# Products on constants ahead of the first projections: five before the first transposes, twenty-four in place of fourteen, and seven more between the turns of the first tile

## The chip, the cores and the metric

The kernel runs on one core of one Trainium2 chip. The metric is the device time of one execution in microseconds (us). A core has five engines that run their own instruction queues: TensorE (PE, whose weight loads stand apart as PEld), VectorE (DVE), ScalarE (ACT), GpSimd (POOL) and SyncE (SP). SP here does nothing but issue loads and stores. Instructions of different engines wait for each other through semaphores.

## The reference

One layer of a decoder trunk, with 512 positions and 1024 channels, in fp32. Cut to what matters here:

```python
cs = jax.nn.silu(c)
mod = cs @ w_ada[l] + b_ada[l]
shift1, scale1, gate1, shift2, scale2, gate2 = ... jnp.split(mod, 6, axis=-1)

h = _rmsnorm(x, norm1_g[l]) * (1.0 + scale1) + shift1
proj = h @ w_in[l]
qa, ka, va, qd, kd, vd, ga, gd = jnp.split(proj, points, axis=-1)
out_a = _sliding_window_attention(qa, ka, va, swa_sinks[l], slopes_swa)
out_d = _diff_attention(qd, kd, vd, lam, lam_init, diff_subln_g[l], slopes_diff)
merged = sigmoid(ga) * (out_a @ w_branch_swa[l]) + sigmoid(gd) * (out_d @ w_branch_diff[l])
x = x + gate1 * (merged @ w_out[l])

h2 = _rmsnorm(x, norm2_g[l]) * (1.0 + scale2) + shift2
x = x + gate2 * _conv_ffn(h2, w_up[l], conv_w[l], conv_b[l], w_down[l])
return _rmsnorm(x, final_g)
```

`mod` is a product of one row with a 1024 x 6144 matrix. The change lies ahead of the first 768 columns of `h @ w_in`, which are `qa`, `ka` and `va`.

## The kernel before

**Products.** An fp32 operand is split in two parts, high and low, of the type fp32r; a product is made of three: high x high, low x high, high x low. ScalarE makes the high part by a copy, VectorE the low part by a subtraction. So each weight that is loaded costs one instruction on ScalarE and one on VectorE: `w0h` and `w0l` (L297 to L306) for the first projections, `w_h` and `w_l` (L115, L116) for those of the heads.

**PSUM** is given out from pools: two banks "f", three "s", two "t" and one "v". The six accumulators of the first projections, `acc6`, take two f, three s and the v. `acc6[5]` is the v.

**The start** (L230 to L415) stands under a manual schedule for VectorE, ScalarE and TensorE: their instructions keep the order in which they are written. SP's queue is ordered by the scheduler, by times that it plans. Step by step:

- `crow`, eight rows of `c`, is loaded and transposed on TensorE (L164); `cs = silu(c)` follows on ScalarE and VectorE (L232 to L235).
- `rows` (the bias of the modulation, the gains of the norms) comes through ScalarE's queue and is transposed on TensorE (L237).
- `keep_warm(WARM)` (L337 to L342): 14 products of `ident` and `ones` into `acc6[5]`, which the first real product overwrites. No one reads them.
- `ac_ops` (L246 to L258): VectorE sums the columns of `w_ada`, each of its eight row blocks times a column of `cs`, into two halves `ac`, and adds the two (L258). `reduce_mod` (L260 to L268) sums over the partitions on TensorE: `pa`, four matmul records. `finish_mod` (L270 to L278) makes the scale and shift `mod` of 128 channels from it (L274, L277).
- `stat`, `normalise`, `turn` for the four row tiles of x: sum of squares on ScalarE (L349), the reciprocal root on VectorE and GpSimd (L169 to L183), the scaling of the first 256 channels (L356), and the transposition of the first 128 channels on TensorE (L361). Behind the first three turns stands a `keep_warm(3)` each, behind the first one also `finish_mod(0, reduce_mod(0))`.
- `h_tile` (ScalarE, L318) applies `mod` to the transposed tile, `h_low` (VectorE, L322) makes its low part.
- The loop over eight groups of 128 channels of h: `mm_k` (L324 to L334) has three parts of six products. While group g is multiplied, VectorE and ScalarE prepare group g+1: its weights (`split_hi`, `split_lo`), its column sums and `mod`, its turn and tile of h. `pa` of the next group stands on TensorE ahead of the third part.

**Behind it** (`man.close()`, L416) TensorE alone keeps a written order. VectorE, ScalarE and SP are ordered by the scheduler, by the times that it plans and by priorities. What runs there first:

- the accumulators are taken out as `qa` (ScalarE L431, VectorE L432), `ka` (L428, L429) and `vaT`;
- `lp`, `ls`, `nlam` (L460 to L464) and `nsink` (L466), small ones on VectorE, from the loads `lamv` and `sink`; `cv` (L454) from the transposed `crow` of the convolution;
- `load_cols` (L469 to L472) loads the heads' weights `w` and splits them;
- `ada_rows` (L757 to L785) makes the other four rows of modulation: 32 loads `ra` of 512 KB through SP, two instructions `arow` on VectorE for each (L776 for the first of a row, else L778). The next load is asked for ahead of the sums over the last one, and the loads share four raw buffers with `w`. A row goes through TensorE and ScalarE (`row`, L794) and GpSimd's queue to memory;
- the sliding-window branch, by pairs of heads: scores on TensorE (`sw`), `st` with the maxima on VectorE (L561), `nm` (L572), exponentials on ScalarE (L573 to L577), `lsum` and the scaling of `st` on VectorE (L580 to L584), transposes `tp` (L595) and values `oa` on TensorE. Scores and softmax have a high priority; the sums `arow` have half of it from a certain step of the order on.

After that come the differential branch, the output projection, and the gated MLP, where TensorE works without long pauses up to the end.

Of the kernel before, what the change touches and what calls it, by code (L numbers as in the profile page):

```python
# [14 lines left out]
P = 128  # L15
# [20 lines left out]
NORM_LAG = 16  # L36
SWA_FILL = (2, 2, 5, 2, 2, 2, 2, 3)
DIFF_FILL = (3, 2, 4, 2)
WARM = 14
GROUPS = ((0,), (1,), (2,), (3,), (4,), (5,), (6,), (7,))  # L40
AC_CUT = 7
MOD_AT = 2
# [11 lines left out]
def kernel(  # L54
# [22 lines left out]
    nc = tc.nc  # L77
# [12 lines left out]
    def bank(tag, bufs, shape, name, dt=F32):  # L90
        return ps.tile(shape, dt, tag=tag, bufs=bufs, name=name)
# [7 lines left out]
    def tbank(name, shape=(P, S)):  # L99
        return bank("t", 2, list(shape), name)  # L100
# [28 lines left out]
    ident = cpool.tile([P, P], F32, name="ident")  # L129
    make_identity(nc, ident)  # L130
    ones = cpool.tile([P, P], F32, name="ones")
# [96 lines left out]
    acc6 = {i: (fbank, sbank, vbank)[(0, 0, 1, 2, 1, 1)[i]](f"a{i}") for i in DONE}  # L228
# [5 lines left out]
    nc.vector.reciprocal(cs, cs)  # L234
    nc.vector.tensor_mul(cs, cs, pc8)  # L235
    pc = tbank("pc", (P, NR))
    nc.tensor.transpose(pc, rows, ident[:NR, :NR])  # L237
    cols = cpool.tile([P, NR], F32, name="cols")
    nc.vector.tensor_copy(cols, pc)
# [6 lines left out]
    def ac_ops(gi, lo, hi):  # L246
        g = groups[gi]
        if lo == 0:
            ac[gi] = [pp.tile([P, 2, len(g) * P], F32, tag=f"ac{b}", bufs=2, name=f"ac{gi}_{b}") for b in range(2)]
        aw = adaw[g[0]]  # L250
        for kk in range(lo, hi):
            a = ac[gi][kk % 2]
            if kk < 2:
                nc.vector.tensor_scalar_mul(a, aw[:, :, kk], cs[:, kk : kk + 1])
            else:
                nc.vector.scalar_tensor_tensor(a, aw[:, :, kk], cs[:, kk : kk + 1], a, ALU.mult, ALU.add)
        if hi == KT:
            nc.vector.tensor_add(ac[gi][0], ac[gi][0], ac[gi][1])  # L258

    def reduce_mod(gi):  # L260
        pas = []
        for i, k in enumerate(groups[gi]):
            pa = tbank(f"pa{k}", (P, 2))
            for j in range(2):
                nc.tensor.matmul(
                    pa[:, j : j + 1], ac[gi][0][:, j, i * P : (i + 1) * P], ones[:, 0:1], start=True, stop=True
                )
            pas.append(pa)  # L268
        return pas

    def finish_mod(gi, pas):
        for k, pa in zip(groups[gi], pas):
            m = pp.tile([P, 16], F32, tag="mod", bufs=3, name=f"mod{k}")
            nc.vector.scalar_tensor_tensor(  # L274
                m[:, 0:1], pa[:, 0:1], bsc1[:, k : k + 1], n1g[:, k : k + 1], ALU.add, ALU.mult
            )
            nc.vector.tensor_add(m[:, 1:2], pa[:, 1:2], bsh[:, k : k + 1])  # L277
            mods[k] = m  # L278

    def w0_views(k):  # L280
        wh, wl = wts[k]
        return [
            a.rearrange(f, **n)
            for a, f, n in (
                (w0[k][:, 0:512], "p (a i d) -> p i a d", dict(a=2, i=4)),
                (wh[:, 0:512], "p (i a d) -> p i a d", dict(i=4, a=2)),
                (wl[:, 0:512], "p (i a d) -> p i a d", dict(i=4, a=2)),
            )
        ]

    def split_hi(k):
        pl, nb = (wp, WB) if k % 2 == 0 else (pp, 2)
        wh = pl.tile([P, 768], F32R, tag="whi", bufs=nb, name=f"w0h{k}")
        wl = pl.tile([P, 768], F32R, tag="wlo", bufs=nb, name=f"w0l{k}")
        wts[k] = (wh, wl)
        rq, wq, lq = w0_views(k)
        nc.scalar.copy(wq, rq)  # L297
        nc.scalar.copy(wh[:, 512:768], w0[k][:, 512:768])

    def split_lo(k, part):  # L300
        wh, wl = wts[k]
        if part == 0:
            rq, wq, lq = w0_views(k)
            nc.vector.tensor_tensor(lq, rq, wq.bitcast(F32), ALU.subtract)
        else:
            nc.vector.tensor_sub(wl[:, 512:768], w0[k][:, 512:768], wh[:, 512:768].bitcast(F32))  # L306
# [8 lines left out]
    def h_tile(k):  # L315
        hf = pp.tile([P, S], F32, tag="hf", bufs=2, name=f"hf{k}")
        for dst in (hTh[k], hf):
            nc.scalar.activation(dst, pts[k], AF.Identity, bias=mods[k][:, 1:2], scale=mods[k][:, 0:1])  # L318
        hfs[k] = hf
# [13 lines left out]
                    acc6[i], lhs[:, i * P : (i + 1) * P], rhs[k], start=k == 0 and p == 0, stop=last and p == 2  # L333
                )  # L334


    def keep_warm(n):  # L337
        for i in range(n):
            nc.tensor.matmul(acc6[5][:, :P], ident, ones, start=True, stop=True)

    keep_warm(WARM)
    ac_ops(0, 0, KT)  # L342
    rst = pp.tile([P, NT], F32, name="rst")
    half = [None] * NT

    def stat(t):
        sq = pp.tile([P, D], F32, tag="sq", bufs=1, name=f"sq{t}")
        ss = pp.tile([P, 1], F32, tag="ss", bufs=4, name=f"ss{t}")
        nc.scalar.activation(sq, xn[:, t], AF.Square, accum_out=ss)  # L349
        half[t] = rstd_start(ss, 1, D, pp)  # L350
# [3 lines left out]
    def normalise(t):  # L354
        rstd_end(rst[:, t : t + 1], *half[t], 1, pp)
        nc.vector.tensor_scalar_mul(xn[:, t, :HEAD], xn[:, t, :HEAD], rst[:, t : t + 1])  # L356
# [3 lines left out]
    def turn(t):  # L360
        nc.tensor.transpose(pts[0][:, t * P : (t + 1) * P], xn[:, t, 0:P], ident)  # L361

    for t in range(NT):
        stat(t)
        if t:
            normalise(t - 1)
            turn(t - 1)
            keep_warm(3)
        if t == 1:
            finish_mod(0, reduce_mod(0))  # L370
    split_hi(0)
    normalise(NT - 1)
    turn(NT - 1)
    h_tile(0)
    split_lo(0, 0)
    split_lo(0, 1)
# [491 lines left out]
    for s in range(4 * DIFF_HEADS):  # L868
        h, n = divmod(s, NT)
# [947 lines left out]
```

## Time and profile before

| what | value |
|---|---|
| median of 3 runs | 703.3 us (701.72 to 703.88) |
| the profiled execution's own time | 702.35 us |
| its span in the profile | 700.5 us |
| mean granted TensorE clock | 0.995 |
| loads `ra`, median from issue to landing | 3.9 us |

A line of the timeline gives the start, the duration, the engine, the line of the code, the operation, what it writes and reads, and in brackets the idle time ahead of it on its engine with what ended it. A line that stands for several instructions has their number at its end. Times begin with the span. A granted clock of 1.00 is the full clock of TensorE. An engine's idle time costs something only where the chain of waits that sets the end runs through it.

### The profile page before, as it was taken

The numbers are of one execution on the slowest core, as the hardware profiler recorded it, in microseconds if no ns is written. First come the engines' busy times: TensorE is split into PE (matmuls) and PEld (weight loads), VectorE is DVE, ScalarE is ACT, GpSimd is POOL, SyncE is SP. The second block draws the span as 40 slices with busy tenths as digits, with TensorE's granted clock in tenths as the row PEclk, the third lists the DMA queues.
The fourth block names the chain that finished last, engine by engine and source line by source line (L and its number), as shares of the span: only waits on it lengthen the run. The fifth ranks groups of instructions, "written<-read, shape, count | busy, mean of one in ns | idle before, by whom it ended". The sixth has DMA issues, their size and how long they took to land.

```text
span 700.5 us, 11253 instructions
## 1 busy us (share of the span) xinstructions
PE 682.6 (97%) x4203; PEld 595.0 (85%) x4203; DVE 573.1 (82%) x1100; ACT 375.1 (54%) x666; POOL 82.4 (12%) x100
## 2 busy tenths in 40 slices
PE   6999999999999999999999999999999999999995
PEld 5777777777788888888889999999999999888884
DVE  5999886887985656663589999888888999979996
ACT  4646666454552333332468656655555666656664
POOL 3000000000001000000030111112111102540300
PEclk9999999999999999999999999999999999999998
DMA  9995454354535676239717788786889738997903
GB/s 313 289 273 159 149 152 151 98 173 121 140 102 160 207 232 185 91 99 281 251 39 144 151 200 199 174 209 184 209 213 217 173 129 219 191 198 196 166 1 120
DMA packets 115862, 121.81 MB, mean 174 GB/s; under 512 B 4383, under 2 KB 93280, under 8 KB 115808
## 3 DMA queue, kind: packets, MB, share of 16 engines
q1 hardware_dynamic: 96894, 95.09, 43.4%
q0 software_dynamic: 18720, 25.73, 22.0%
q8 instruction: 33, 0.54, 0.3%
q10 hardware_dynamic: 194, 0.28, 0.1%
q14 instruction: 21, 0.17, 0.1%
HBM read 118.97 MB, written 2.11 MB: 173 GB/s over the span
## 4 chain that ended last, share of the span: by engine, by line
PE 75%; DVE 13%; DMA 4%; ACT 4%; issue 2%; SPq 0%; POOL 0%; POOLq 0%; ACTq 0%
PE up L1152 26%; PE dc L1761 13%; DMA ra<-in_w_ada_dram 4%; PE a L332 3%; PE pgd L119 2%; PE oc L1208 2%; PE oc L1212 2%; PE pgd L121 2%; PE oc L1209 2%; PE pgd L120 2%; PE pga L119 2%; PE pga L121 2%; PE pga L120 2%; DVE arow L778 1%; DVE m_wlo L1097 1%
## 5 line engine op out<-in xcount | busy, mean ns | idle before, releaser
L1152 PE MATMUL up<-t,m_whi 128*128 128x256 f32 x528 | 96.2, 283 | 0.0
L1152 PEld LDWEIGHTS up<-t,m_whi 128*128 128x128 f32 x528 | 82.3, 192 | 0.0
L1152 PE MATMUL up<-t,m_wlo 128*128 128x256 f32 x264 | 74.7, 284 | 0.5 <-DVE m_wlo L1097 0.5
L1152 PE MATMUL up<-bh,p_wlo 128*128 128x256 f32 x232 | 65.6, 283 | 0.1
L1152 PE MATMUL up<-bh,p_whi 128*128 128x256 f32 x232 | 65.6, 283 | 0.0
L1152 PE MATMUL up<-bl,p_whi 128*128 128x256 f32 x232 | 65.6, 283 | 0.0
L778 DVE SCALAR_TENSOR_TENSOR arow<-ra,cs,arow 128x512 f32<-128x512 f32 x56 | 41.9, 749 | 21.0 <-DMA ra<-in_w_ada_dram 20.5
L1152 PEld LDWEIGHTS up<-t,m_wlo 128*128 128x128 f32 x264 | 50.6, 192 | 0.9 <-DVE m_wlo L1097 0.9
L1152 PEld LDWEIGHTS up<-bh,p_wlo 128*128 128x128 f32 x232 | 44.5, 192 | 0.3 <-DVE p_wlo L1097 0.3
L1152 PEld LDWEIGHTS up<-bl,p_whi 128*128 128x128 f32 x232 | 44.5, 192 | 0.0
L1152 PEld LDWEIGHTS up<-bh,p_whi 128*128 128x128 f32 x232 | 44.5, 192 | 0.0
L1065 POOL DMA_DIRECT2D s<-in_w_up_dram x21 | 27.0, 1360 | 143.1 <-DMA s<-in_w_up_dram 54.2
L1097 DVE TENSOR_TENSOR m_wlo<-s,m_whi 128x1024 fp32r<-128x1024 f32 x31 | 37.7, 1217 | 0.9 <-ACT m_whi L1093 0.9
L1093 ACT CAST m_whi<-s 128x1024 fp32r<-128x1024 f32 x31 | 32.4, 1047 | 9.6 <-DVE s L1087 6.2
L1152 PE MATMUL up<-t,p_whi 128*128 128x256 f32 x176 | 32.3, 284 | 0.5 <-DVE pairs L1192 0.5
L173 POOL TENSOR_TENSOR r<-ms,mhalf 128x1 f32<-128x1 f32 (+1 forms) x16 | 12.7, 796 | 133.1 <-DVE ms L171 74.1
L795 POOL DMA_DIRECT2D mod_rows<-row x8 | 5.1, 642 | 197.4 <-ACT row L794 197.4
L1152 PEld LDWEIGHTS up<-t,p_whi 128*128 128x128 f32 x176 | 27.4, 192 | 0.7 <-issue 0.7
L698 ACT ACTIVATE sd<-sd,dmx 128x128 f32<-128x128 f32 (+3 forms) x32 | 17.7, 557 | 19.0 <-DVE dmx L690 18.8
L1159 ACT ACTIVATE gT<-a,cv 128x512 f32<-128x512 f32 x22 | 17.7, 813 | 17.7 <-DVE a L1194 17.3
L1093 ACT CAST p_whi<-wa 128x1024 fp32r<-128x1024 f32 x18 | 18.7, 1041 | 12.0 <-PE up L1152 7.2
L1152 PE MATMUL up<-t,p_wlo 128*128 128x256 f32 x88 | 24.9, 283 | 0.0
(473 smaller groups left out, 2053.6 us busy)
## 6 DMA issues: line engine op xcount, KB each, us to landing
ra<-in_w_ada_dram SPq DMA_DIRECT2D x32, 512.0 KB, 3.9
wa<-in_w_up_dram SPq DMA_DIRECT2D x22, 512.0 KB, 4.0
s<-in_w_up_dram SPq DMA_DIRECT2D x21, 512.0 KB, 4.7
s<-in_w_up_dram POOLq DMA_DIRECT2D x21, 512.0 KB, 6.9
adaw<-in_w_ada_dram SPq DMA_DIRECT2D x16, 512.0 KB, 5.4
w<-in_w_in_dram SPq DMA_DIRECT2D x12, 512.0 KB, 3.9
a<-in_w_up_dram SPq DMA_DIRECT2D x11, 512.0 KB, 4.7
b<-in_w_down_dram SPq DMA_DIRECT2D x10, 512.0 KB, 3.8
```

Of the source, the lines that this page charges most:

```text
L119: nc.tensor.matmul(o, lh, rh, start=start, stop=False)
L120: nc.tensor.matmul(o, lh, rl, start=False, stop=False)
L121: nc.tensor.matmul(o, ll, rh, start=False, stop=stop)
L332: nc.tensor.matmul(acc6[i], lhs[:, i * P : (i + 1) * P], rhs[k], start=k == 0 and p == 0, stop=last and p == 2)
L698: exp = nc.scalar.activation(pm[m], pm[m], AF.Exp, bias=mx[:, m : m + 1], scale=slope, accum_out=lsum[:, m : m + 1])
L778: nc.vector.scalar_tensor_tensor(ac, r[:, a], cc, ac, ALU.mult, ALU.add)
L1065: nc.gpsimd.dma_start(dst, upblock(*blk), accum_op=ALU.add)
L1093: nc.scalar.copy(W[J, name][0], R[J, SRC[name]])
L1097: nc.vector.tensor_sub(lo, R[J, SRC[name]], hi.bitcast(F32))
L1152: nc.tensor.matmul(o[u], w[:, k, cu], b[:, k], start=name in ("p1", "m5", "p2") and k == 0 and x == 0, stop=k == 3 and x == 2, skip_group_ ...
L1159: nc.scalar.activation(grow(j), av[J][:, u], AF.Identity, bias=cv[:, 66 + j : 67 + j], scale=cv[:, 44 + j : 45 + j])
L1761: nc.tensor.matmul(bank2[u][:, sl], a[:, q, cu], b[:, q, sl], start=first_mm and x == 0, stop=last_mm and x == 2, skip_group_check=name no ...
```

## The change

`keep_warm` is defined further up, ahead of the transpose of `rows`, and is called at four places:

- five products (`WARM_EARLY`) ahead of that transpose, behind the one of `c`;
- `WARM` is 24 in place of 14, ahead of the first column sums;
- five behind `finish_mod(0, reduce_mod(0))`, ahead of the second turn;
- two behind the fourth turn.

That is 22 products more, each of two passes. They write `acc6[5]` like the others and add no wait on TensorE. The rest of the code is the same; TensorE's order, too, but for these products.

The planned times of the scheduler shift with them, and so do queues that it orders:

- **SP:** the loads of `sink`, `lamv`, the two `crow` and of the fifth `w` of the first projections go ahead of the column loads of group 3; the first loads `ra` stand behind the buffers of the first heads' weights.
- **VectorE and ScalarE:** `lp`, `ls`, `nlam` and `nsink` come some groups earlier. The first split of a head's weights, `w_h` and `w_l`, comes earlier: `w_l` stands between the last `ac` sum and the addition L258 of the last group, where `ls` stood.
- **VectorE behind the groups:** before, the order is four of `qa` and `ka`; `arow` 1 to 3; four `st`; `arow` 4; four `st`; two `nm`; one `qa`; `w_l`; `arow` 5; `lsum`; `arow` 6. After, it is `arow` 1 and 2; three of `qa` and `ka`; `arow` 3; one `qa`; `arow` 4; four `st`; `arow` 5; four `st`; two `nm`; `arow` 6; one `qa`; `w_l`; `lsum`. Further on, `qkv` goes behind the next scores and `arow` 7, and `arow` 8 ahead of the next `w_l`. The orders are the same again behind that.

```diff
--- before.py
+++ after.py
@@ -36,7 +36,8 @@
 NORM_LAG = 16
 SWA_FILL = (2, 2, 5, 2, 2, 2, 2, 3)
 DIFF_FILL = (3, 2, 4, 2)
-WARM = 14
+WARM_EARLY = 5
+WARM = 24
 GROUPS = ((0,), (1,), (2,), (3,), (4,), (5,), (6,), (7,))
 AC_CUT = 7
 MOD_AT = 2
@@ -234,6 +235,13 @@
     nc.vector.reciprocal(cs, cs)
     nc.vector.tensor_mul(cs, cs, pc8)
     pc = tbank("pc", (P, NR))
+
+
+    def keep_warm(n):
+        for i in range(n):
+            nc.tensor.matmul(acc6[5][:, :P], ident, ones, start=True, stop=True)
+
+    keep_warm(WARM_EARLY)
     nc.tensor.transpose(pc, rows, ident[:NR, :NR])
     cols = cpool.tile([P, NR], F32, name="cols")
     nc.vector.tensor_copy(cols, pc)
@@ -333,11 +341,6 @@
                     acc6[i], lhs[:, i * P : (i + 1) * P], rhs[k], start=k == 0 and p == 0, stop=last and p == 2
                 )
 
-
-    def keep_warm(n):
-        for i in range(n):
-            nc.tensor.matmul(acc6[5][:, :P], ident, ones, start=True, stop=True)
-
     keep_warm(WARM)
     ac_ops(0, 0, KT)
     rst = pp.tile([P, NT], F32, name="rst")
@@ -368,9 +371,11 @@
             keep_warm(3)
         if t == 1:
             finish_mod(0, reduce_mod(0))
+            keep_warm(5)
     split_hi(0)
     normalise(NT - 1)
     turn(NT - 1)
+    keep_warm(2)
     h_tile(0)
     split_lo(0, 0)
     split_lo(0, 1)
```

## The prediction

> **What bounds the kernel now.** The page comes first: its span, its busy shares, the granted clock in 40 slices, and the chain that ended last.
>
> ```profile
> span 700.5 us, 11253 instructions
> ...
> PE 682.6 (97%) x4203; PEld 595.0 (85%) x4203; DVE 573.1 (82%) x1100; ACT 375.1 (54%) x666; POOL 82.4 (12%) x100
> ...
> PEclk9999999999999999999999999999999999999998
> ...
> PE 75%; DVE 13%; DMA 4%; ACT 4%; issue 2%; SPq 0%; POOL 0%; POOLq 0%; ACTq 0%
> ```
>
> TensorE is busy for 97% of the span and carries three quarters of the chain. The slices are 17.5 us long, so a cold stretch of a few microseconds cannot be seen in them. The busy time by windows shows it (after the window: the sum, then PE, PEld, DVE, ACT and POOL busy, granted clock, DMA share, GB/s):
>
> ```profile
> 14.00:16.00 2.00, 1.36 (x7) 1.36 (x8) 1.71 (x10) 0.47 (x2) 1.32 (x2) 0.55 1.11 372
> 16.00:18.00 2.00, 2.00 (x13) 2.00 (x13) 2.00 (x6) 0.03 (x1) 0.00 (x0) 0.59 1.13 350
> 18.00:20.00 2.00, 1.57 (x9) 1.15 (x8) 2.00 (x6) 2.00 (x4) 0.00 (x0) 1.00 1.11 371
> ```
>
> For about 3.5 us the clock is near one half, and it is full again from 18. That is the stretch the added products aim at. What it costs is read on the engine that waits. The timeline of VectorE has these waits for the sum `pa`, which TensorE makes (start, duration, instruction, idle before and its releaser):
>
> ```profile
> 13.53 0.22 DVE L274 SCALAR_TENSOR_TENSOR mod<-pa,cols 128x1 f32<-128x1 f32 x1 [1.44 <-PE pa L265]
> 22.21 0.22 DVE L274 SCALAR_TENSOR_TENSOR mod<-pa,cols 128x1 f32<-128x1 f32 x1 [0.38 <-PE pa L265]
> 27.70 0.22 DVE L274 SCALAR_TENSOR_TENSOR mod<-pa,cols 128x1 f32<-128x1 f32 x1 [0.30 <-PE pa L265]
> 33.03 0.22 DVE L274 SCALAR_TENSOR_TENSOR mod<-pa,cols 128x1 f32<-128x1 f32 x1 [0.16 <-PE pa L265]
> ```
>
> The first wait stands ahead of the cold stretch. Those at 22.21 and 27.70 are 0.22 and 0.14 longer than the 0.16 of the steady rhythm. In between VectorE is full (1.71 and twice 2.00 in the windows above), and its column sums set the pace of the projections. So a warm TensorE at 14 to 18 us can bring 0.22 + 0.14 = **0.36 us**, and no more.
>
> **The change, part 1: the products.** The timeline of TensorE and of the first tile of h:
>
> ```profile
> 2.40 0.24 PE L164 MATMUL pc<-ident,crow 8*128 8x8 f32 x1 [2.40 <-DMA crow<-in_c_dram]
> 4.80 0.27 PE L237 MATMUL pc<-ident,rows 25*128 25x25 f32 x1 [2.17 <-DMA rows<-in_diff_subln_g_dram]
> 5.00 6.14 PE L339 MATMUL a<-ones,ident 128*128 128x128 f32 x28
> 12.15 0.33 PE L361 MATMUL xt<-ident,xn 128*128 128x128 f32 x1 [1.02 <-DVE xn L356]
> 12.32 0.83 PE L339 MATMUL a<-ones,ident 128*128 128x128 f32 x6
> 12.99 0.50 PE L265 MATMUL pa<-ones,ac 128*128 128x1 f32 x4
> 14.64 0.47 PE L361 MATMUL xt<-ident,xn 128*128 128x128 f32 x1 [1.15 <-DVE ms L169]
> ```
>
> ```profile
> 17.97 0.78 ACT L318 ACTIVATE hThA<-xt,mod 128x512 fp32r<-128x512 f32 x1 [3.50 <-PE xt L361]
> ```
>
> A product is two passes (14 products are 28 records). The 28 passes took 6.14, 0.219 each; the six at 12.32 took 0.67 to the start of the next, 0.111 each. So the clock rose between 11.0 and 12.3, that is 6.2 to 7.5 us after TensorE began to run without a pause at 4.80.
>
> Early five: 10 x 0.219 = 2.19 from 2.64, so to 4.83, where the next transpose started at 4.80 after a wait of 2.17 for its load. That wait hides them; without this cover they would cost 2.19.
>
> Twenty-four in place of fourteen: 48 passes from 5.03. If the clock rises 6.2 to 7.5 us after 2.64, at 8.84 to 10.14, then 17.4 to 23.3 passes are slow and the rest take 0.111: the end is 12.2 to 12.9. The transpose at 12.15 waits for VectorE until then, and behind it stand `pa` and VectorE's wait of 1.44. So this part is **0.1 to 0.7 late**, and I take 0.3: the rise is nearer to its early bound if the run is counted from the transpose at 2.40. If the clock does not rise at all, the end is 5.03 + 48 x 0.219 = 15.5, 3.4 late.
>
> The Trainium skill, "TensorE: Matmul & The Clock Gate", Part 1, section "What's actually happening", says that the clock is decided on free-running windows of about 3.41 us, not on a count of products. By that rule an estimate of the rise is between one and two such windows after 2.64, at 6.1 to 9.5, and this part would be up to 0.4 late, so the sum below would be up to 0.3 lower. The cold stretch of about one window's length in the rows above agrees with the rule; the 6.2 to 7.5 measured at the start lies at its upper end and beyond.
>
> Five after `pa`: 10 x 0.111 = 1.1 in the pause of 1.15 ahead of 14.64, hidden; cold they would reach 1.0 past it, which would come off the 3.50 that ScalarE waits at 17.97. Two after the fourth turn: 4 x 0.111 = 0.44 behind the transposes, before h has been made (0.78): hidden, 0.88 if cold. I take zero for both. Part 1 with the gain: −0.36 + 0.3, about **0** (from −0.26 to +0.34).
>
> **Part 2: what the scheduler moves.** The queues of SP, VectorE and ScalarE are planned, and 22 more products shift the plan. On SP, four small loads (`sink`, `lamv` and both `crow`) and the fifth `w` of the projections go ahead of the column loads of group 3, into a time when those wait for buffers in any case; I count nothing for it. If it did hold up group 3, each small load would cost about one issue. On VectorE, three moves count. The rows around the end of the projections:
>
> ```profile
> 53.16 0.28 DVE L461 TENSOR_REDUCE ls<-lp 128x2 f32<-128x128 f32 x1
> 53.36 0.41 DVE L258 TENSOR_TENSOR ac<-ac,ac 128x256 f32<-128x256 f32 x1
> ...
> 55.14 1.22 DVE L116 TENSOR_TENSOR w_l<-w,w_h 128x1024 fp32r<-128x1024 f32 x1
> 56.27 0.24 DVE L454 COPY cv<-pcv 128x88 f32<-128x88 f32 x1
> ...
> 58.78 0.75 DVE L432 SCALAR_TENSOR_TENSOR qa<-a,qsc,qa 128x512 fp32r<-128x512 f32 x1 [0.48 <-ACT qa L431]
> ```
>
> ```profile
> 53.92 0.58 PE L265 MATMUL pa<-ones,ac 128*128 128x1 f32 x4
> ```
>
> (a) The first split `w_l` takes the place of `ls` ahead of the last addition of `ac` (L258). It occupies 56.27 − 55.14 = 1.13, `ls` 53.36 − 53.16 = 0.20, so the addition, the last `pa`, the last projections and with them `qa` come **0.93** later. Queued behind it on VectorE: the `mod` that TensorE's last eighth waits for. The 0.48 that VectorE idles at 58.78 is no cover, since it waits there for that same chain. I take 0.9: the first `qa` at 59.68.
>
> (b) The sums `arow` over the loads `ra` are put elsewhere. Before, from the first `qa` on:
>
> ```profile
> 61.37 0.47 DVE L776 TENSOR_SCALAR arow<-ra,cs 128x512 f32<-128x512 f32 x1
> 61.88 1.54 DVE L778 SCALAR_TENSOR_TENSOR arow<-ra,cs,arow 128x512 f32<-128x512 f32 x2
> 63.33 0.28 DVE L561 CUSTOM_DVE_ANT_0 st<-sw,dsw 128x128 f32<-128x128 f32 x1
> ...
> 64.44 0.74 DVE L778 SCALAR_TENSOR_TENSOR arow<-ra,cs,arow 128x512 f32<-128x512 f32 x1
> 65.11 0.41 DVE L561 CUSTOM_DVE_ANT_0 st<-sw,dsw 128x256 f32<-128x256 f32 x1
> ...
> 66.74 0.74 DVE L432 SCALAR_TENSOR_TENSOR qa<-a,qsc,qa 128x512 fp32r<-128x512 f32 x1
> ...
> 68.81 0.75 DVE L778 SCALAR_TENSOR_TENSOR arow<-ra,cs,arow 128x512 f32<-128x512 f32 x1 [0.19 <-DMA ra<-in_w_ada_dram]
> ...
> 76.34 0.75 DVE L778 SCALAR_TENSOR_TENSOR arow<-ra,cs,arow 128x512 f32<-128x512 f32 x1 [0.19 <-DMA ra<-in_w_ada_dram]
> ```
>
> and the chain has these loads between them:
>
> ```profile
> 65.21 3.58 DMA ra<-in_w_ada_dram
> ...
> 70.38 5.94 DMA ra<-in_w_ada_dram
> ...
> 78.26 3.92 DMA ra<-in_w_ada_dram
> ```
>
> After the change, two `arow` go ahead of the `qa`, and the third and fourth among them. The third load is issued when the fourth `arow` has ended, as before (65.11, issue 65.21). It ends at 59.68 + 2.59 (the four of `qa` and `ka`, 58.78 to 61.37) + 1.45 (two `arow`, 61.88 to 63.33) = 63.72, the load is issued at 63.82 and lands at 67.40 with the 3.58 of the chain. But the fifth `arow`, which needs it, now stands ahead of the second four `st`, where before those four, `nm`, a `qa` and a `w_l` were in between. VectorE has only the first four `st` (64.44 − 63.33 = 1.11) until then, is free at 64.83, and **idles for 2.57** where it idled for 0.19. Behind that wait stand the scores' `st` and `nm`, for which ScalarE's exponentials wait, then TensorE's transposes of `st`. Then 0.67 for the `arow` (65.11 − 64.44) and 66.74 − 65.11 = 1.63 for `st` and `nm`: done at 69.70 instead of 66.74, 2.96 late.
>
> (c) From there VectorE catches up. Before, 66.74 to 76.34 is 9.60; of this fall away the two waits of 0.19 and the fifth `arow` (0.67), so 8.55 is left. The seventh and eighth `arow` follow (1.34), and the eighth now stands ahead of the next `w_l`: end at 69.70 + 8.55 + 1.34 = 79.59. `qkv` is moved inside this stretch, net zero. The next `ra` is issued behind it at 79.69, against 78.26: **1.43 late**. The load that took 5.94 is issued at about 70.4 as before and has landed long before it is needed at 78.3.
>
> Is this slip hidden afterwards? The rows that follow:
>
> ```profile
> 82.20 0.49 DVE L776 TENSOR_SCALAR arow<-ra,cs 128x512 f32<-128x512 f32 x1 [1.91 <-DMA ra<-in_w_ada_dram]
> ```
>
> ```profile
> 111.19 1.12 PE L595 MATMUL tp<-ident,st 128*128 128x128 f32 x7 [0.65 <-ACT row L794]
> ```
>
> VectorE waits for that load at 82.20, so its slip is passed on. The sums go on in the same order as before until they give the row that TensorE waits for at 111.19. That idle time is no cover, since it ends with the late chain; it grows.
>
> **Sum.** 0 + 1.43 = +1.4. Against the profiled execution's own time, 702.35 (its span 700.5 and 1.85 around it), that is 703.8. The profiled execution lies 0.95 under the median of the runs, 703.3, so on that scale the forecast is **704.7**.
>
> **The rivals.**
>
> *The third `ra` takes as long as the fourth* (slower). Place: the wait of VectorE behind the first four `st`. The chain has 3.58, 5.94 and 3.92 for such loads; with 5.94 the wait grows by 2.36 and the sum is +3.8: **707.1**. It decides from about 4.3 us on, where the sum passes 2.1. For it: `w` loads are issued close by. Against it: the like load at 65.21 had them too and took 3.58.
>
> *The longer run stays cold* (the change doesn't do what it says): TensorE is at half clock through all 48 passes, the first transpose is 3.4 late, and with part 2 the sum is −0.36 + 3.4 + 1.4 = +4.4: **707.7**. Against it: the rise came 6.2 to 7.5 us after the start, and the run is 10 us long.
>
> *The slip is regained.* Between 82 and 111 us further loads of this kind follow; if each is issued as a buffer comes free and some of them land in 3.58 instead of up to 5.94, the 1.4 can be made good and only the gain at the start is left: 702.35 − 0.36, **702.9** on the median's scale. Against it: the chain runs through VectorE there too, with the same instructions.
>
> *Ordinary executions are colder than the profiled one.* The runs span 701.72 to 703.88; if the difference is the clock's phase ahead of the projections and the warm run removes it, all executions come at the fastest run's time less 0.36, 701.4; without the slip and with a transpose that is no longer late it could be **701.1**. Nothing in one profile shows this. The free-running window that the Trainium skill states in the same section would be a ground for it.
>
> **How the numbers follow.** The forecast has a chance of 0.56; its own range is 704.3 to 705.7 (part 1 from −0.26 to +0.34, the load from 3.58 to 3.92, further moves some tenths). The slow load has 0.14, the cold run 0.07, the regained slip 0.15, the colder executions 0.08. A measurement of this kernel can tell 0.3%, 2.1 us, from no change: below 701.2 and above 705.4. Of the forecast's 0.56 I put 0.39 under that and 0.17 over it. So faster 0.08, same 0.39 + 0.15 = 0.54, slower 0.17 + 0.14 + 0.07 = 0.38. The range of 702.4 to 707.1 holds the forecast, the regained slip and the slow load, and leaves out the two others, 0.15.
>
> **What would show it.** Part 1: clock 1.00 in the windows from 14 to 18, the passes from 5 us on turning from 0.22 to 0.11 at 8.8 to 10.1, the first transpose at 12.2 to 12.9, and waits for `pa` of 0.16 in place of 0.38 and 0.30. Part 2: the last `ac` addition some 0.9 later than before, an idle time of about 2.6 ahead of the fifth `arow`, the row at 82.20 some 1.4 later, and the transpose of 111.19 as much. The forecast is wrong if VectorE waits for another engine in the steady groups, if the fifth `arow` finds its load landed, or if the slip at 83 us is no longer there at 111.

## The result and the profile after

The changed kernel takes 705.92 us (median of 6 runs, 704.61 to 707.0); the kernel before, run beside it, 702.79 us (6 runs, 701.72 to 703.88). The ratio is 1.0043, with a 95% interval of 1.003 to 1.0056: 3.1 us **slower**. The profiled execution of the changed kernel took 706.81, one of its slower ones, with a span of 704.7.

The page of the changed kernel, its busy shares and its chain of waits by engine:

```profile
PE 687.2 (98%) x4247; PEld 598.0 (85%) x4247; DVE 573.3 (81%) x1100; ACT 375.2 (53%) x666; POOL 82.4 (12%) x100
...
PE 73%; DVE 15%; DMA 5%; ACT 3%; issue 2%; POOL 0%; SPq 0%; POOLq 0%; DVEq 0%; ACTq 0%
```

TensorE has 44 records more and 4.6 us more busy time, and the span is 4.2 longer. It would be easy to read the one as the cause of the other. But the chain has moved from TensorE to VectorE and the DMA (15% and 5% in place of 13% and 4%), not to TensorE. So the stages are looked at one after the other.

The windows that were cold before, in the changed kernel:

```profile
14.00:16.00 2.00, 2.00 (x17) 1.82 (x17) 1.78 (x10) 0.54 (x2) 1.37 (x2) 1.00 1.14 374
16.00:18.00 2.00, 2.00 (x18) 1.78 (x16) 1.91 (x7) 0.76 (x2) 0.00 (x0) 1.00 1.10 352
```

The clock is at 1.00 where it was 0.55 and 0.59. The products do what they are there for. The timeline of TensorE shows the starts:

```profile
2.57 2.50 PE L242 MATMUL a<-ones,ident 128*128 128x128 f32 x10
5.01 0.30 PE L245 MATMUL pc<-ident,rows 25*128 25x25 f32 x1
5.24 6.96 PE L242 MATMUL a<-ones,ident 128*128 128x128 f32 x48
12.64 0.33 PE L364 MATMUL xt<-ident,xn 128*128 128x128 f32 x1 [0.44 <-DVE xn L359]
```

The 48 passes end at 12.20, and the transpose behind them waits another 0.44 for VectorE: the longer run is hidden. That this transpose starts 0.49 later than before comes from VectorE, whose first columns arrived later. On VectorE:

```profile
14.02 0.22 DVE L282 SCALAR_TENSOR_TENSOR mod<-pa,cols 128x1 f32<-128x1 f32 x1 [1.44 <-PE pa L273]
22.48 0.22 DVE L282 SCALAR_TENSOR_TENSOR mod<-pa,cols 128x1 f32<-128x1 f32 x1 [0.16 <-PE pa L273]
27.90 0.22 DVE L282 SCALAR_TENSOR_TENSOR mod<-pa,cols 128x1 f32<-128x1 f32 x1 [0.16 <-PE pa L273]
...
28.96 0.62 DVE L262 TENSOR_SCALAR ac<-adaw,cs 128x256 f32<-128x256 f32 x2 [0.44 <-DMA adaw<-in_w_ada_dram]
...
53.91 1.22 DVE L117 TENSOR_TENSOR w_l<-w,w_h 128x1024 fp32r<-128x1024 f32 x1
55.05 0.42 DVE L266 TENSOR_TENSOR ac<-ac,ac 128x256 f32<-128x256 f32 x1
```

The waits for `pa` are down to 0.16, so the gain has come. A wait that was not there before stands at 28.96, for the columns of group 3 (the groups count from 0; the expectations below call it the third group), and `w_l` holds the last addition back. The chain of waits has the load of these columns, and the `ra` behind the projections (start, duration, what):

```profile
21.71 7.15 DMA adaw<-in_w_ada_dram
...
58.00 5.21 DMA ra<-in_w_ada_dram
...
65.41 3.86 DMA ra<-in_w_ada_dram
...
82.10 3.94 DMA ra<-in_w_ada_dram
```

Behind the projections, on VectorE:

```profile
63.31 0.75 DVE L783 SCALAR_TENSOR_TENSOR arow<-ra,cs,arow 128x512 f32<-128x512 f32 x1 [0.83 <-DMA ra<-in_w_ada_dram]
...
69.36 0.75 DVE L783 SCALAR_TENSOR_TENSOR arow<-ra,cs,arow 128x512 f32<-128x512 f32 x1 [2.87 <-DMA ra<-in_w_ada_dram]
...
71.67 0.74 DVE L783 SCALAR_TENSOR_TENSOR arow<-ra,cs,arow 128x512 f32<-128x512 f32 x1
...
75.91 0.16 DVE L585 TENSOR_TENSOR lsum<-lsum,es 128x4 f32<-128x4 f32 x1 [0.30 <-ACT st L581]
...
86.06 0.49 DVE L781 TENSOR_SCALAR arow<-ra,cs 128x512 f32<-128x512 f32 x1 [1.47 <-DMA ra<-in_w_ada_dram]
```

The fifth `arow` waits 2.87 for its load with the second four `st` queued behind it; ahead of that, the third waits 0.83, and later the second `lsum` 0.30 for the exponentials that started late. TensorE, which had waited for nothing there, now waits for that chain:

```profile
74.87 1.23 PE L600 MATMUL tp<-ident,st 128*128 128x128 f32 x7 [0.77 <-DVE st L589]
77.83 0.98 PE L600 MATMUL tp<-ident,st 128*128 128x128 f32 x7 [0.34 <-ACT pT L602]
81.46 0.50 PE L120 MATMUL pw<-hThA,w_h 128*128 128x512 f32 x1 [0.58 <-DVE qkv L437]
...
115.36 1.12 PE L600 MATMUL tp<-ident,st 128*128 128x128 f32 x7 [0.64 <-ACT row L799]
```

The transpose that was at 111.19 is at 115.36, 4.17 later, and the idle time ahead of it is the same, 0.64 and 0.65. Nothing of the slip is regained; from there to the end of the span both kernels take 589.3.

**A table by stages** makes the executions comparable, since the start of the first sums moves by up to 1.1 us from one execution to the next, with and without the change. It is read from VectorE's and TensorE's timelines: A is from the first `mod` (13.53 before) to the last (54.53), B from there to the first sum of the next row (82.20), C from there to the transpose that waits for `row` (111.19). For the kernel before A is 41.00, B 27.67, C 28.99.

| kernel | A | B | C | wait for adaw in A | ratio to before, interval |
|---|---|---|---|---|---|
| before | 41.00 | 27.67 | 28.99 | none | 1 |
| changed | 42.21 | 29.83 | 29.30 | 0.44 | 1.0043 (1.003 to 1.0056) |
| e7, changed again | 42.66 | 29.64 | 28.78 | 0.90 | 1.0051 (1.0037 to 1.0064) |
| e1, all products, old queues | 40.65 | 27.81 | 29.05 | none | 1.0006 (0.9998 to 1.0015) |
| e4, seven products only | 40.65 | 27.58 | 28.90 | none | 0.9998 (0.9989 to 1.0007) |
| e2, new queues, no products | 41.86 | 28.93 | 28.99 | none | 1.0032 (1.002 to 1.0043) |
| e3, sixth sum back | 41.67 | 28.95 | 28.78 | none | 1.0035 (1.0023 to 1.0048) |
| e6, fifth sum back | 41.68 | 28.02 | 28.81 | none | 1.0019 (1.001 to 1.0028) |
| e10, SP's order and early w_l | 41.67 | 27.24 | 28.79 | none | 1.0008 (0.9999 to 1.0016) |
| e9, SP's order alone | 42.32 | 27.78 | 28.88 | 1.14 | 1.0008 (0.9998 to 1.0019) |
| e5, both back by the planner | 40.94 | 29.20 | 28.92 | 0.18 | 1.0029 (1.0017 to 1.0041) |
| e8, sums earlier | 40.65 | 29.09 | 29.50 | none | 1.0010 (1.0001 to 1.0019) |
| e11, eight products | 41.00 | 27.36 | 28.82 | none | 1.0013 (1.0004 to 1.0022) |

The stages belong to one execution each, the ratios to 5 to 12 runs beside 6 to 29 of the kernel before; they can differ a little from the quotient of the medians given below. Of the 4.17 in the two profiles, 0.49 lies ahead of A, 1.21 in A, 2.16 in B and 0.31 in C. The 0.49 is the landing of the first columns: the first sums begin at 6.47 to 6.61 in eleven of the thirteen profiled executions, and only before (7.10) and changed (7.60) are later.

### The profile page after: what moved, and what is told of

It reads as the page before. It is cut to its first block, busy times and chain, and to the rows that moved or that the text cites. A ratio compares the mean times of both kernels' runs of the same rounds, so it can differ in the third digit from the quotient of the medians.

```text
span 704.7 us, 11339 instructions
## 1 busy us (share of the span) xinstructions
PE 687.2 (98%) x4247; PEld 598.0 (85%) x4247; DVE 573.3 (81%) x1100; ACT 375.2 (53%) x666; POOL 82.4 (12%) x100
## 4 chain that ended last, share of the span: by engine, by line
PE 73%; DVE 15%; DMA 5%; ACT 3%; issue 2%; POOL 0%; SPq 0%; POOLq 0%; DVEq 0%; ACTq 0%
PE up L1157 26%; PE dc L1766 13%; DMA ra<-in_w_ada_dram 4%; PE pgd L120 2%; PE oc L1213 2%; PE oc L1214 2%; PE pgd L122 2%; PE oc L1217 2%; PE pgd L121 2%; DMA adaw<-in_w_ada_dram 2%; PE a L340 2%; PE pga L120 2%; PE pga L122 2%; PE pga L121 2%; DVE ac L264 1%
```

## The experiments

The theory: the products cost nothing, and the queues that they shift cost it all, on VectorE behind the projections above all. The rival: the products cost the time by themselves.

**All products, old queues (e1).** SP's first loads are put under a written order, the one they had before. VectorE's order then comes out as before, with no further edit.

```diff
-    for g in groups:
-        if g[0]:
-            load_ada(g)
-        for k in g:
-            r = raw_tile([P, 768], f"w0_{k}")
-            nc.sync.dma_start(r, win[k * P : (k + 1) * P, 0:768])
-            w0[k] = r
+    with tc.manual_schedule(engines={nc.sync.engine}):
+        load_ada(groups[0])
...
+        load_w0(2)
+        load_w0(3)
+        load_ada(groups[3])
+        load_w0(4)
+        load_w0(5)
+        load_ada(groups[4])
...
+        load_ada(groups[7])
```

> All 22 products are there; the order of SP's first loads is written out as it was before the change, and VectorE's order then comes out as before, too (one load of a head's weight stays a place earlier on SP, and its high-part copy on ScalarE). Theory, that the queues lose the time and not the products: the last ac addition near 53.4 us (+-0.5), at most 0.5 us of idle time ahead of the fifth arow, and 702.2 to 703.5 us, ratio to before 0.999 to 1.001. Rival, that the products cost the time by themselves (a late first transpose, TensorE occupied): 705 to 706.5 us, ratio 1.003 to 1.005.

Measured: 702.14 us beside 701.64. The 22 products with the old queues cost nothing that can be told from zero (at most 1.1 us by the interval), and the stage behind the projections is as before (27.81).

**New queues, no products (e2).** The same edit on the kernel before, with the order that SP has after the change (`w` 4, `sink`, `lamv` and `crow` ahead of group 3's columns, and so on).

> None of the 22 products; SP's first loads are written out in the order that they have after the change, and VectorE's order behind the projections comes out as after it. Theory (queues): cold stretch at 14 to 18 us as before, last ac addition some 1 to 1.7 us later than before, 2.5 to 3 us of idle time ahead of the fifth arow, and 705 to 706.5 us, ratio 1.003 to 1.006. Rival (products): 702.3 to 703.5 us.

Measured: 703.9 us, +2.3, of the 3.1 that the whole change cost (3.2 when it was run again, e7). So the queues by themselves cost most of it. The rest is not placed: the intervals of the ratios overlap, and e1 leaves room for a part of the products. VectorE's timeline shows the stall without a single added product:

```profile
64.09 0.42 DVE L574 CUSTOM_DVE_ANT_0 st<-sw,dsw 128x256 f32<-128x256 f32 x1
67.23 0.75 DVE L791 SCALAR_TENSOR_TENSOR arow<-ra,cs,arow 128x512 f32<-128x512 f32 x1 [2.72 <-DMA ra<-in_w_ada_dram]
67.90 0.42 DVE L574 CUSTOM_DVE_ANT_0 st<-sw,dsw 128x256 f32<-128x256 f32 x1
```

Four `st`, 2.72 of nothing, one `arow`, and only then the other four `st`, whose scores had been ready. One part of the expectation was wrong: no cold stretch came. The clock was 1.00 from 14 to 18 us in this execution, without the products:

```profile
14.00:16.00 2.00, 1.95 (x16) 1.83 (x17) 1.78 (x8) 0.00 (x0) 0.73 (x2) 1.00 1.11 380
16.00:18.00 2.00, 1.57 (x9) 1.18 (x8) 2.00 (x7) 1.84 (x3) 0.00 (x0) 1.00 1.14 346
```

So the products may buy less than 0.36 us on average, since an execution without them can be warm, too. Here the first columns had landed sooner, and TensorE paused for 0.67 ahead of the first transpose, in place of 1.02 before; whether that kept the clock up was not tried.

**The sums' priority (e3).**

```diff
-ADA_EASY = 20
+ADA_EASY = 32
```

> The changed kernel, but the sums over the second and third ra have no raised priority, so that the fifth arow stands behind the first softmax's nm, the fourth qa and a w_l again; SP's queue and the early w_l stay as changed. If the wait of 2.87 ahead of the fifth arow is what costs most: idle ahead of it under 1 us, slip at the next ra about 1 to 2 in place of 3.9, 703.5 to 704.5 us. Rival, that the late start of the chain (early w_l, SP's loads) costs it all: 705 us and more.

Measured: 704.23, ratio 1.0035. A miss of the edit: it moved the sixth `arow` back, and the third behind the last of the four `qa` and `ka`, where it no longer waits; the fifth stayed ahead of the second four `st`, with an idle time of 2.97. So it says nothing of the fifth. Stage B is as long as in e2 (28.95 and 28.93), where the third and the sixth stand as changed, so no gain from moving these two is seen.

**Seven products only (e4).** `WARM_EARLY` 0, `WARM` 14, the other two calls as changed.

> Only the seven products between the turns, with 14 ahead of them and none early; all queues as before. If they alone hold the clock: 1.00 in the windows from 14 to 18 us, waits for pa at 22 and 28 us near 0.16, and 0.2 to 0.4 us less than before (702.3 to 702.8). If a cold stretch comes in spite of them: clock near 0.55 somewhere from 13 to 19 us, and the time of before within 0.4 us. Rival, that ordinary executions are colder than the profiled one: 701.3 us or less.

Measured: 701.45 beside 701.64, ratio 0.9998. The clock is 1.00 from 14 to 18 us, stage A is 40.65, 0.35 less than in the profile of before. The times cannot tell this from zero. The rival with colder ordinary executions falls: a warm run does not bring 2 us.

**The fifth sum back (e6).** In the changed kernel it is issued behind the `nm` of the first softmax; `nms` is that instruction.

```diff
-                        nc.vector.scalar_tensor_tensor(ac, r[:, a], cc, ac, ALU.mult, ALU.add)
+                        with tc.issue_after(pairs[0].nms.ins) if (idx, hf, k, a) == (0, 0, 4, 0) else ExitStack():
+                            nc.vector.scalar_tensor_tensor(ac, r[:, a], cc, ac, ALU.mult, ALU.add)
```

> The changed kernel with all products, its SP queue and the early w_l, but the fifth arow is issued behind the nm of the first softmax (the planner moves qkv back with it). If the wait of the fifth arow ahead of the scores is worth what the trace says: idle ahead of it under 0.8 us, the next ra some 1 us earlier than in the changed kernel, and ratio to before 1.001 to 1.002, which is the early w_l's 0.9 us and what SP costs. Rival, that the wait only moves to another place: ratio 1.003 or more, as in the changed kernel.

Measured: 702.86, ratio 1.0019, beside 1.0051 for the changed kernel on the same chip. VectorE:

```profile
65.07 0.42 DVE L566 CUSTOM_DVE_ANT_0 st<-sw,dsw 128x256 f32<-128x256 f32 x1
65.90 0.42 DVE L566 CUSTOM_DVE_ANT_0 st<-sw,dsw 128x256 f32<-128x256 f32 x1 [0.40 <-PE sw L127]
...
68.18 0.75 DVE L784 SCALAR_TENSOR_TENSOR arow<-ra,cs,arow 128x512 f32<-128x512 f32 x1 [0.55 <-DMA ra<-in_w_ada_dram]
```

The load is as late as ever; but the `st` and the `nm` now run while it is under way, and 0.55 of the wait is left. One sum in another place, with what moved along (the sixth `arow`, `qkv` and the eighth `arow`), is worth 1.8 us by the medians against the changed kernel on the same chip (702.86 and 704.69), 2.2 by the ratios (0.0032 of 702). Not all of that need be the sum: of the two profiled executions only the changed kernel's (e7, below) has the wait for group 3's columns, and stage A differs by 0.98, stage B by 1.62. Against e3, whose profile has no such wait either, the gain is 0.93 in stage B and 1.1 by the ratios. So the place of the sum is worth one to two microseconds.

**The changed kernel again (e7).**

> The changed kernel once more, on the same chip as the other runs. Ratio to before 1.003 to 1.0056 as in the first comparison. Its second profile tells whether the first column load landing at 7.6 us and the wait of 0.44 for the third group's columns come every time (both theories of SP's part: systematic, seen again; by chance, gone and the slip at the next ra nearer 2 us than 4).

Measured: 704.69 beside 701.44. VectorE's waits for group 3's columns and for the third `ra`:

```profile
28.83 0.61 DVE L262 TENSOR_SCALAR ac<-adaw,cs 128x256 f32<-128x256 f32 x2 [0.90 <-DMA adaw<-in_w_ada_dram]
...
69.15 0.75 DVE L783 SCALAR_TENSOR_TENSOR arow<-ra,cs,arow 128x512 f32<-128x512 f32 x1 [3.12 <-DMA ra<-in_w_ada_dram]
```

The late first columns are gone (they came by chance), the wait for group 3's columns is there again, and twice as long.

**Both back, by the planner (e5).** In the changed kernel the first `w_l` is issued behind the last `mod`.

```diff
-        nc.vector.tensor_sub(lo, src, hi.bitcast(F32))
+        with tc.issue_after(held.pop().ins) if held else ExitStack():
+            nc.vector.tensor_sub(lo, src, hi.bitcast(F32))
...
-            nc.vector.tensor_add(m[:, 1:2], pa[:, 1:2], bsh[:, k : k + 1])
+            held[:] = [nc.vector.tensor_add(m[:, 1:2], pa[:, 1:2], bsh[:, k : k + 1])]
```

> The changed kernel with all products and its SP queue, but the first w_l is issued behind the last mod; the planner then also puts the fifth arow behind all eight st and the nm. If VectorE's two moves are the loss: ratio to before 0.999 to 1.001, last mod within 0.2 us of the 41.0 us that it came after the first mod before the change. If SP's earlier small loads cost in themselves: a wait for adaw of 0.4 us or more in the groups, ratio 1.001 or more.

Measured: 703.28, ratio 1.0029, a miss. Stage A is good (40.94), but the planner (the scheduler that orders the queues) found a third order: the first four `arow` ahead of all eight `st`. TensorE then waits 0.55 for VectorE to free the scores' banks, VectorE for the scores (0.61) and for the third `ra` (1.28), and stage B is 29.20.

**The sums earlier (e8)**, on the kernel with the seven products: `ADA_EASY = 12`.

> The kernel before with only the seven products between the turns, and the raised priority of the arow sums from the first one on (12 in place of 20): the first four arow go between and behind the first qa, then all eight st and the nm without a break, then the fifth. If the chain of ra loads sets the pace behind the projections: the third ra is issued 1 to 2 us earlier, no idle time over 0.5 us ahead of the fifth arow, 0.5 to 2 us less than before (ratio 0.997 to 0.9995). Rival, that VectorE's own work sets it: ratio 0.9995 to 1.001.

Measured: 702.03, ratio 1.0010. The same kind of order as in the last one, made on purpose, and no gain. TensorE's timeline has a wait that fits:

```profile
63.23 0.38 PE L127 MATMUL sw<-ka,qa 64*128 64x256 f32 x1
64.41 0.97 PE L127 MATMUL sw<-ka,qa 64*128 64x256 f32 x11 [0.80 <-DVE mx L566]
```

With four sums in front, the `st` that free the scores' banks are late, and TensorE waits. The order of before, with three sums, then four `st`, then the fourth, lies between the two faults.

**SP's order alone (e9).** All products and SP's order as changed; the first `w_l` held behind the last `mod` as above, the fourth `arow` behind the first four `st` (`four`), the fifth behind the third `w_l` (`lows[2]`), as they stood before.

```diff
+                        behind = {(0, 0, 2, 1): four, (0, 0, 4, 0): lows[2]}.get((idx, hf, k, a))
+                        with tc.issue_after(behind.ins) if behind else ExitStack():
+                            nc.vector.scalar_tensor_tensor(ac, r[:, a], cc, ac, ALU.mult, ALU.add)
```

> The changed kernel with all products and its SP queue; the first w_l, the fourth and the fifth arow are held in the places that they had before the change, and VectorE's order is the one of before but for the small lp, ls, nlam and nsink, which stay early. What is left is SP's share (and the products'). If the earlier small loads delay the third group's columns: a wait for adaw of 0.2 to 0.9 us near 28 us, last mod 41 to 41.6 us after the first, ratio to before 1.0003 to 1.0015. If SP's order costs nothing: 40.65 us, no such wait, ratio 0.9990 to 1.0003.

Measured: 702.07 beside 701.85, ratio 1.0008 (0.9998 to 1.0019). The profiled execution was the longest of its twelve (704.3), and there group 3's columns came 1.14 late:

```profile
29.73 0.62 DVE L265 TENSOR_SCALAR ac<-adaw,cs 128x256 f32<-128x256 f32 x2 [1.14 <-DMA adaw<-in_w_ada_dram]
```

Of the eight profiled executions with SP's changed order four have this wait (0.18 to 1.14); of the five with the old order none has it. Four of the twelve runs took 703.4 to 704.3, the other eight 701.0 to 702.4; one of these four was profiled, and it has the wait. This fits a cost of SP's order in some executions, and little in the median; that the wait is behind all four is not shown.

**The early `w_l` with it (e10).** The same without the hold on `w_l`.

> As the run of SP's share, but the first w_l stands ahead of the last ac addition as in the changed kernel (the planner then also leaves the first two arow ahead of the qa). The difference of the two is the early w_l: 0.9 to 1.1 us at the last mod. If that delay is passed on to the end: ratio to before 1.0012 to 1.0028. If the time behind the projections swallows it: within 0.0005 of the other.

Measured: 702.24, ratio 1.0008 (0.9999 to 1.0016), the same as without. Stage A is 41.67, so the early `w_l` costs its 1.02 against 40.65 there; but stage B is 27.24, 0.54 less than with `w_l` in its old place. On VectorE the first two `arow` now run ahead of the `qa`:

```profile
58.18 0.49 DVE L783 TENSOR_SCALAR arow<-ra,cs 128x512 f32<-128x512 f32 x1 [0.18 <-DMA ra<-in_w_ada_dram]
58.70 0.75 DVE L787 SCALAR_TENSOR_TENSOR arow<-ra,cs,arow 128x512 f32<-128x512 f32 x1
59.71 0.75 DVE L439 SCALAR_TENSOR_TENSOR qa<-a,qsc,qa 128x512 fp32r<-128x512 f32 x1 [0.25 <-ACT qa L438]
```

They fill a time in which VectorE would have waited for `qa`. About half of the delay is given back. The fifth `arow`, behind the ready work again, finds its load landed:

```profile
69.58 0.75 DVE L787 SCALAR_TENSOR_TENSOR arow<-ra,cs,arow 128x512 f32<-128x512 f32 x1
```

This run has all the products, SP's changed order and the early `w_l`. Only the fourth and the fifth sum, and what moves along, stand as before, and the ratio falls from 1.0051 to 1.0008. That is the plainest evidence for the cause.

**Eight products (e11)**, none of the added ones: `WARM` 8.

> The kernel before with eight products on constants in place of fourteen ahead of the first column sums and none of the added ones; all queues as before. TensorE then pauses for 3 us and more ahead of the first transpose and has a slow clock in the turns. If VectorE's sums set the pace and a cold TensorE costs little: waits for pa at 22 and 28 us of 0.3 to 0.8 in sum more than 0.16 each, 0.2 to 1.0 us more than before (ratio 1.0003 to 1.0015). Rival, that the clock ahead of the projections sets their time: 2 us and more (ratio 1.003).

Measured: 702.63 beside 701.85, ratio 1.0013. The windows:

```profile
12.00:14.00 2.00, 2.00 (x11) 2.00 (x11) 0.00 (x0) 1.85 (x6) 0.00 (x0) 0.50 1.14 346
14.00:16.00 2.00, 0.85 (x5) 0.77 (x5) 1.52 (x10) 0.29 (x1) 1.07 (x2) 0.50 1.10 378
16.00:18.00 2.00, 2.00 (x11) 2.00 (x11) 1.86 (x7) 0.00 (x0) 0.29 (x1) 0.50 1.14 348
```

Half clock for more than six microseconds, through all the turns, costs 0.8 us by the medians and 0.9 by the ratio: the first `mod` waits 2.49 for `pa` in place of 1.44, and stage A has 0.35 more than a warm one. That is the size of what warmth can be worth in this stage.

## Why the prediction came out as it did

The direction was right and the place, too; the size was half of what came: +1.4 forecast, +3.1 measured, 704.7 and 705.92. The measured time lies above the forecast's own range, which ended at 705.7, and inside the wide one of 702.4 to 707.1, which reached that far to hold another rival, the slow third load. That load did not come. So the mechanism was right and its sum too small, and that the wide range holds the result is in part luck.

*The gain of 0.36: right in size.* The waits at 22 and 28 us went to 0.16, and stage A is 40.65 in the warm kernels with the old order, 0.35 less than before. Not seen was that an execution without the products can be warm as well (e2), and that the profile before was an unusual one, with its first columns late.

*The end of the 48 passes at 12.2 to 12.9, 0.3 late: its lower bound, and hidden.* They ended at 12.20, and the transpose waited another 0.44 for VectorE. The ten early passes took 2.44, not 2.19, so that the next transpose came at 5.01 in place of 4.80 and the 48 passes began 0.21 later than worked out; this was hidden as well. The forecast set 12.15 as a fixed time; it is the time of VectorE's first tile, which moves with the landing of the first columns. The clock rose sooner than the 8.8 to 10.1 us forecast, which the one start of before had given. In the changed kernel's windows the count of passes goes from 6 to 9 at about 8.0, which is 5.4 after 2.57:

```profile
7.20:8.00 0.80, 0.80 (x6) 0.80 (x6) 0.40 (x2) 0.00 (x0) 0.00 (x0) 1.00 1.09 384
8.00:8.80 0.80, 0.80 (x9) 0.80 (x9) 0.80 (x3) 0.03 (x1) 0.00 (x0) 1.00 0.93 343
```

The Trainium skill, "TensorE: Matmul & The Clock Gate", Part 1, section "What's actually happening", has free-running windows of about 3.41 us; the estimate of one to two windows that the prediction made from it, 6.1 to 9.5, holds this 8.0.

*(a) The early `w_l`, 0.93: right at its place* (1.02 in stage A, e3, e6 and e10 against e1), *not seen as a term of the sum*. By itself it costs nothing that the times can tell (e10 with it and e9 without it are both at 1.0008, each known to about 0.7 us). In the profiles the sums that move up into the wait for `qa` give half of it back.

*(b) An idle time of 2.57 ahead of the fifth `arow`: right* (2.87, again 3.12, and 2.72 without products). That it is the main cause is shown by e6, where that one sum in another place takes back one to two microseconds, and by e10, where with the fourth sum put back too the ratio is 1.0008.

*(c) The catching up behind it, and so the 1.43: the step that failed.* Against 27.67 the forecast had 0.5 more in stage B (1.43 less the 0.9 of the `w_l`); measured were 2.16, 1.97 and, without products, 1.26. Three things were not priced. The third `arow` waits for its own load, 0.83, 0.50 and 0.28: the forecast took it as landed. The third `ra` takes 3.86 in the changed kernel's chain (4.11 the second time), not 3.58. And from the end of the `nm` to the next `ra`'s issue it took 10.43 (71.67, when the next `arow` starts, to 82.10) in place of the 9.99 worked out, mostly the 0.30 that the second `lsum` waits for ScalarE: the exponentials stand behind the late `nm`, which the forecast named and did not price. These three make 0.83 + 0.28 + 0.44 = 1.55 of the 1.66 by which stage B was longer than forecast. Why the second `ra` was quicker in e2 (4.66 in its chain, 5.21 and 4.88 in those of the changed kernel) is not settled.

*SP's loads, counted at nothing: wrong in some executions.* Group 3's columns came 0.44 and 0.90 late, with a `w` and the 128 KB of `lamv` put in front of them. The forecast looked at when these columns are issued, and that did not change (21.29 against 20.80, the delay of the first `mod`); it did not ask what is still under way ahead of them. So one of its own signs of being wrong came in part: in the groups VectorE waited for a load, though not for another engine. Of the two `crow` only the first stands ahead of these columns; the second is issued behind them, at 24.79.

*No cover behind: right.* The slip at 82 us was there at 111 in every kernel; stage C is 28.8 to 29.5.

*The rivals.* The slow third load did not come: 3.86 and 4.11 lie under the 4.3 from which it was to decide, and far from 5.94. The regained slip, the cold run and the colder executions fell. No version tried is faster than the kernel before; the seven products alone are level with it.

## What to carry to other kernels

In a kernel whose queues are planned, an edit in the pauses of one engine can also be an edit of the queues of others: compare the orders first, and price what moved before what was added. A wait at the head of an in-order queue costs what is queued behind it: ask of each load whose consumer moved up when it is issued, when it lands, and what ready work then stands behind. And a stage is worth warming only where its engine is what the others wait for; here more than six cold microseconds cost 0.9, and a sum in the wrong place one to two.

## What was not expected of the hardware

The granted clock reads 1.00 in the windows from 7.2 to 8.8 us above, on both sides of the step from 6 to 9 passes: at the start of an execution the column did not show the slow clock, and the rate of equal instructions had to be counted. The step also moves between executions of one kernel. In the second profile of the changed kernel it comes about a microsecond sooner, near 7 us, 4.4 after TensorE's start:

```profile
6.40:7.20 0.80, 0.80 (x7) 0.80 (x6) 0.69 (x3) 0.00 (x0) 0.00 (x0) 1.00 1.02 353
7.20:8.00 0.80, 0.80 (x9) 0.80 (x9) 0.80 (x3) 0.00 (x0) 0.00 (x0) 1.00 1.00 394
```

In the profile of before it came more than 6.2 us after the start.

A load of 512 KB of columns took from its issue to its use 7.15 us in the chain above and 8.29 in that of e9, where the median of such loads in the first 60 us of before is 5.4. Which of the loads ahead of it delays it, if any, was not tried.
